# A trunk layer on one Trainium2 core: the ninth pair's up products as seven products, one side's sums kept behind the last head, and the eleventh pair's low parts by DMA

## The chip, the cores and the metric

The kernel runs on one NeuronCore of a Trainium2 chip. The core's engines work side by side, each through its own queue in order: TensorE (PE) multiplies matrices, with PEld its weight loads; VectorE (DVE) does elementwise work; ScalarE (ACT) copies, scales and applies functions; GpSimd (POOL) does small elementwise work and issues some transfers; SyncE (SP) issues most DMA transfers. Engines wait for each other by semaphores. SBUF is the on-chip memory of 128 partitions, PSUM the small memory that TensorE writes, DRAM the memory outside.

The metric is the time of one execution in microseconds. Before the change three runs took 644.28 to 644.42 us, median 644.31.

## The reference

One decoder layer over 512 tokens of width 1024, in float32: forgetting attention with 16 heads, a layer norm, a feed-forward part whose gate passes a causal convolution, a second layer norm, and a gated embedding. The part that is changed is the feed-forward part:

```
def conv_ffn(x, w_up, conv_w, conv_b, w_down):
    u, g = jnp.split(x @ w_up, [FFN_DIM], axis=-1)
    g = causal_dwconv(g, conv_w, conv_b)
    return (jax.nn.gelu(g, approximate=False) * u) @ w_down
```

FFN_DIM is 2816, that is 22 blocks of 128 columns. All blocks, and the 16 heads before them, are computed in both kernels.

## The kernel before, in words

**Split products.** Every float32 operand is cut into a high part (a copy in TensorE's rounded format, whi, xh, written by ACT at L123) and a low part (the operand minus the high part, wlo, xl, written by VectorE at L129). Each product is three matmuls: high with high, high with low, low with high (`three`, L147). The weights pass through class `Weights` (L64): a unit is 1024 columns per partition; `load_to` loads it into a buffer called raw from SP's queue (some units go into a spare piece of another tile, shown as side in the trace), `cut_to` cuts it into whi and wlo, five buffers of each, and `get` asks for a unit and cuts up to four units ahead. With by_dma set (L124), ACT writes the negated high part into wlo, and a DMA from POOL's queue adds the weights to it; VectorE has no part in it.

**Attention.** `scores` (L540) makes a head's probabilities in a tile pr of 1280 columns, of which there are two, used in turn; `turn` (L578) transposes them on TensorE, `values` (L593) multiplies with the values. In the last steps, `out_first` (L615) starts the output projection. `keep_load` and `keep_sums` (L474, L488) work beside the heads: they load the two blocks of up weights of one pair and side, make four sums of them on VectorE, and store those in a DRAM tile called kept, for use in the feed-forward part.

**Feed-forward part.** The 22 blocks f are taken in pairs j = f // 2, counted from 0 here as in the code: j = 8 is the ninth pair, j = 10 the eleventh. A plain pair takes four products of 1024x128 weights with 512 tokens: gate and up (g and u, q = 0 and 1) for each of two blocks. A pair in UP_PAIRS is treated as a 2x2 block matrix product, which by Strassen's method in Winograd's form needs seven products of blocks instead of eight; `up_step` (L836) has the four steps st 0 to 3 for each side, with matmuls of 256 tokens. Its operands are sums of weight blocks. They are either made on VectorE when the weights come in (t12, t3, t4 at L199 to L225) or, for a pair in KEPT, loaded ready-made from the kept tiles. Step 0 leaves a sum in PSUM; VectorE adds a saved part to it (L866), and only then may step 1 write the same PSUM bank again.

**Down products.** The products E of a pair are cut into operands for the down product, which is also done in Strassen's form for three pairs at a time (parts 0 to 2: pairs 0 to 2, 3 to 5, 6 to 8). `operand_sums` (L892) makes four sums on VectorE, `operand_parts` (L904) the high and low parts a, b and s. For a pair j whose successor is in APART, these stand inside the next pair (L990 to L993), otherwise at the pair's own end. The twelve chunks of a part's down product are done between the steps of the following three pairs; CHUNKS says how many chunks stand in which slot. Chunks of part 2 stand in pairs 9 and 10.

**What sets the order.** From f = 2 to the end of the loop, VectorE and ACT run in an order written out by hand (L971); in the rest, and on the other engines, a scheduler of the framework sets the order from priorities and its own costs. The trace's PE names: g and u for the up products, x, y and z for the down products' PSUM banks, o for values, ao and ap for the output projection.

## Time and profile before

| | |
|---|---|
| median of the runs | 644.31 us (644.28 to 644.42, 3 runs) |
| the profiled execution's own time | 644.6 us |
| its span, first to last instruction | 642.9 us |
| TensorE busy | 636.6 us |
| VectorE busy | 540.7 us |
| ScalarE busy | 389.4 us |
| GpSimd busy | 129.1 us |
| mean granted TensorE clock | 0.999 |

In a row of a timeline stand the start and the duration in us, the engine, the line, the operation, out<-in, and the shape; in brackets, how long the engine was idle before, and what ended that. A row of the chain of waits has the start, the time and the engine with what it wrote, several equal ones merged. A row of the windows gives each engine's busy time with its number of instructions in the order PE, PEld, DVE, ACT, POOL, then the granted clock, the DMA share and GB/s. Buffer numbers are left out of the names.

### The profile page before, as it was taken

To read this page: it belongs to the slowest core of one execution; us is meant where nothing else is said; L and a number is where in the kernel's file an instruction comes from. 1 tells how busy PE (TensorE), PEld (TensorE's weight loads), DVE (VectorE), ACT (ScalarE), POOL (GpSimd) and SP (SyncE) were. 2 spreads that over 40 slices of the span, in tenths; PEclk is the share of its full clock that TensorE was granted. 3 is DMA by queue.
4 is the path that set the end of the run, shared out by engine and by line. 5 is a ranking of instruction groups with operands and counts; after the bars stand their busy time and mean duration, and the time that the engine had idled before them with its cause. 6 is when DMAs were issued, how large, how long until landed. Compare 5 with 4: busy or idle time off the path is not lost.

```text
span 642.9 us, 10251 instructions
## 1 busy us (share of the span) xinstructions
PE 636.6 (99%) x3707; PEld 562.4 (87%) x3707; DVE 540.7 (84%) x864; ACT 389.4 (61%) x690; POOL 129.1 (20%) x149
## 2 busy tenths in 40 slices
PE   9999999999999999999999999999999999999997
PEld 7899888888888889989999999999988998888886
DVE  7577779988888689857889989999986998599996
ACT  6273787877785316956666566756644455236872
POOL 2000464454456043110000000102020001002001
PEclk9999999999999999999999999999999999999999
DMA  8766634554588777694676868675854774662632
GB/s 316 249 225 211 220 105 166 175 193 152 181 280 295 269 258 204 147 252 137 197 224 154 239 183 275 189 234 168 255 152 123 207 246 100 181 232 73 221 108 98
DMA packets 51666, 126.87 MB, mean 197 GB/s; under 512 B 5088, under 2 KB 8160, under 8 KB 51616
## 3 DMA queue, kind: packets, MB, share of 16 engines
q1 hardware_dynamic: 46384, 111.93, 52.1%
q0 software_dynamic: 5088, 14.16, 11.3%
q8 instruction: 29, 0.48, 0.3%
q14 instruction: 21, 0.17, 0.1%
q10 hardware_dynamic: 144, 0.13, 0.1%
HBM read 111.39 MB, written 20.97 MB: 206 GB/s over the span
## 4 chain that ended last, share of the span: by engine, by line
PE 92%; DVE 4%; issue 1%; DMA 1%; POOL 0%; SPq 0%; ACT 0%; DVEq 0%; POOLq 0%
PE u L152 17%; PE g L152 17%; PE pp L152 13%; PE x L152 8%; PE pl L152 7%; PE pv L152 7%; PE z L152 4%; PE r L152 3%; PE o L600 3%; PE ao L152 3%; PE t L587 3%; PE y L152 2%; PE s L550 2%; PE s L552 2%; PE p L152 1%
## 5 line engine op out<-in xcount | busy, mean ns | idle before, releaser
L123 ACT ACTIVATE whi<-raw 128x1024 fp32r<-128x1024 f32 (+4 forms) x131 | 128.9, 987 | 92.2 <-PE pv L152 18.4
L129 DVE TENSOR_TENSOR wlo<-raw,whi 128x1024 fp32r<-128x1024 f32 (+4 forms) x126 | 141.7, 1129 | 26.7 <-ACT whi L123 26.0
L574 POOL TENSOR_SCALAR pr<-pr,rl 128x128 f32<-128x128 f32 (+1 forms) x64 | 75.6, 1197 | 74.7 <-DVE rl L570 74.7
L283 POOL COPY neghalf<-neghalf 128x1 f32<-128x1 f32 x16 | 9.6, 601 | 244.3 <-ACT neghalf L282 244.3
L152 PE MATMUL g<-x1h,whi 128*128 128x256 f32 (+1 forms) x164 | 51.7, 315 | 0.0
L152 PE MATMUL g<-x1l,whi 128*128 128x256 f32 (+1 forms) x164 | 51.6, 315 | 0.0
L152 PE MATMUL g<-x1h,wlo 128*128 128x256 f32 (+1 forms) x164 | 51.5, 314 | 0.0
L152 PE MATMUL pp<-xh,wlo 128*128 128x512 f32 (+1 forms) x130 | 50.5, 390 | 0.0
L152 PE MATMUL pp<-xh,whi 128*128 128x512 f32 (+1 forms) x130 | 50.5, 388 | 0.1
L152 PE MATMUL pp<-xl,whi 128*128 128x512 f32 (+1 forms) x130 | 50.4, 388 | 0.0
L152 PE MATMUL u<-x1l,whi 128*128 128x256 f32 (+1 forms) x156 | 50.1, 321 | 0.0
L152 PE MATMUL u<-x1h,wlo 128*128 128x256 f32 (+1 forms) x156 | 50.1, 321 | 0.0
L152 PE MATMUL u<-x1h,whi 128*128 128x256 f32 (+1 forms) x156 | 50.1, 321 | 0.0
L566 ACT ACTIVATE pr<-s,nm 128x128 f32<-128x128 f32 (+1 forms) x64 | 33.6, 527 | 11.8 <-DVE nm L562 11.7
L152 PEld LDWEIGHTS g<-x1h,whi 128*128 128x128 f32 x164 | 31.2, 191 | 2.4 <-issue 0.4
L152 PEld LDWEIGHTS g<-x1l,whi 128*128 128x128 f32 x164 | 31.2, 190 | 2.1
L152 PEld LDWEIGHTS g<-x1h,wlo 128*128 128x128 f32 x164 | 31.2, 190 | 1.9
L123 ACT ACTIVATE whi<-side 128x512 fp32r<-128x512 f32 (+1 forms) x32 | 26.4, 828 | 9.3 <-DVE side L216 3.8
L152 PEld LDWEIGHTS u<-x1l,whi 128*128 128x128 f32 x156 | 29.7, 190 | 2.4
L152 PEld LDWEIGHTS u<-x1h,whi 128*128 128x128 f32 x156 | 29.7, 190 | 2.3
L152 PE MATMUL g<-xsh,wlo 128*128 128x256 f32 x112 | 31.7, 283 | 0.0
L152 PE MATMUL u<-xsh,whi 128*128 128x256 f32 x112 | 31.7, 283 | 0.0
(637 smaller groups left out, 1927.7 us busy)
## 6 DMA issues: line engine op xcount, KB each, us to landing
raw<-wup SPq DMA_DIRECT2D x30, 512.0 KB, 4.8
raw<-wdn SPq DMA_DIRECT2D x26, 512.0 KB, 4.8
raw<-wqk SPq DMA_DIRECT2D x14, 512.0 KB, 3.9
ka<-wup SPq DMA_DIRECT2D x10, 512.0 KB
kb<-wup SPq DMA_DIRECT2D x10, 512.0 KB, 4.3
kept<-kb SPq DMA_DIRECT2D x9, 512.0 KB, 3.4
kept<-ka SPq DMA_DIRECT2D x9, 512.0 KB
raw<-wo SPq DMA_DIRECT2D x8, 512.0 KB, 5.1
```

The lines of the kernel that those rows point to most:

```text
L123: self.nc.scalar.activation(hi[:, c:e], piece, AF.Copy)
L129: self.nc.vector.tensor_sub(lo[:, c:e], piece, hi[:, c:e].bitcast(F32))
L152: nc.tensor.matmul(ps, lhsT, rhs, start=start and n == 0, stop=stop and n == 2, skip_group_check=on)
L283: with tc.issue_after(nc.gpsimd.tensor_copy(small[:, m + 32:m + 33], small[:, m:m + 1]).ins):
L550: nc.tensor.matmul(ps[:, :n], QA[:, q], KA[:, :n], start=True, stop=False)
L552: nc.tensor.matmul(ps[:, :n], qb[0:68, q], kb[0:68, :n], start=False, stop=True)
L566: nc.scalar.activation(pr[:, off:off + w], ps[:, :w], AF.Exp, bias=nm[:, i:i + 1], scale=-1.0, accum_out=ls[:, i:i + 1])
L574: nc.gpsimd.tensor_scalar_mul(pr[:, off:off + w], pr[:, off:off + w], rl[:, i:i + 1])
L587: nc.tensor.transpose(ps[:, w:w + P], pr[:, o:o + P], ident)
L600: nc.tensor.matmul(ps[:, q0:], V[:, j, h], p[:, o:o + w], start=j == 0 and n == 0, stop=j == NT - 1 and n == 1)
```

## The change

Four things are done together.

1. Pair 8 joins UP_PAIRS: its four plain products become seven products. Its side q = 0 gets a kept tile; its side q = 1 has its weight sums made on VectorE as they come in. `up_units` now chooses kept or not by side.
2. The kept tile of (8, 0) is the eleventh. Its two weight blocks are loaded after the last head's transposes, into the two buffers of the probabilities, its sums are made on VectorE in the round after that, and stored from SP's queue. The store of the tenth kept tile moves with it.
3. APART gains 8 and 9, so the operand sums and parts of pairs 7 and 8 stand inside pairs 8 and 9.
4. Pair 10 joins DMA_PAIRS: the low parts of its four units are made by ACT and a DMA from POOL's queue.

CHUNKS for part 2 changes from one chunk in each of twelve slots to eight of one, none, one, none or two: the slots of a pair of seven products differ from those of a plain pair.

```diff
-CHUNKS = (None, (1,) * 8 + (0, 1, 2, 1), (1,) * 12, (2, 1) * 4)
-UP_PAIRS = (2, 3, 4, 5, 6, 7, 9)
-KEPT = (3, 4, 5, 6, 7)
-DMA_PAIRS = (1, 2)
-APART = (2, 3, 4, 5, 6, 7)
+CHUNKS = (None,) + ((1,) * 8 + (0, 1, 2, 1),) * 2 + ((2, 1) * 4,)
+UP_PAIRS = (2, 3, 4, 5, 6, 7, 8, 9)
+KEPT = [(j, q) for j in (3, 4, 5, 6, 7) for q in range(2)] + [(8, 0)]
+DMA_PAIRS = (1, 2, 10)
+APART = (2, 3, 4, 5, 6, 7, 8, 9)
@@ up_units(j): kept or not by side
+        def second(q):
+            if (j, q) in KEPT:
+                return W.add(kept[j, q][:, 0:4:3, :], inner=512)
+            return unit(f1, q, t12(wup[f0, 1 - q][:, :4], 3 + q))
+
+        def third(q):
+            if (j, q) in KEPT:
+                return W.add([(kept[j, q][:, 2, :], 512), (wup[f1, 1 - q][:, 4:], 512)])
+            return unit(f1, q, t3)
+
+        def fourth(_):
+            open_ = [q for q in range(2) if (j, q) not in KEPT]
...
+                nc.vector.tensor_sub(v, v, b)
...
+            return W.add([(kept[j, q][:, 1, :] if (j, q) in KEPT else wup[f0, 1 - q][:, 4:], 512)
+                          for q in range(2)], make=make if open_ else None)
@@ keep_load
-    def keep_load(queue=nc.sync):
+    def keep_load(queue=nc.sync, last=False):
...
-            ab = (ap.tile([P, UNIT], F32, name=f"ka{j}_{q}", tag="keep", bufs=1),
-                  base.tile([P, UNIT], F32, name=f"kb{j}_{q}", tag="raw", bufs=RAW_BUFS))
+            if last:
+                ab = [ap.tile([P, 10 * P], F32, tag="pr", name=f"k{c}{j}_{q}")[:, :UNIT] for c in "ab"]
+            else:
+                ab = (ap.tile([P, UNIT], F32, name=f"ka{j}_{q}", tag="keep", bufs=1),
+                      base.tile([P, UNIT], F32, name=f"kb{j}_{q}", tag="raw", bufs=RAW_BUFS))
@@ the loop over the heads
-        elif s == 0:
+        else:
             keep_sums()
-            keep_load()
+            if s:
+                keep_load()
...
         if 1 <= h < H + 1:
             turn(h - 1)
+        if h == H:
+            keep_load(last=True)
```

The engines' instructions change by this: TensorE has 168 matmuls of 256 tokens in pair 8 where it had 96 of 512; VectorE's list of rows grows from 858 to 870, ACT's from 614 to 636. The orders at the three places that the prediction speaks of are shown there.

More of the change, by code (lines that the diff above doesn't have):

```diff
@@ L242, in up_units, with make @@
         f0, f1 = 2 * j, 2 * j + 1
-        if j in KEPT:
-            return (lambda q: W.add(wup[f0, 1 - q], inner=P),
-                    lambda q: W.add(kept[j, q][:, 0:4:3, :], inner=512),
-                    lambda q: W.add([(kept[j, q][:, 2, :], 512), (wup[f1, 1 - q][:, 4:], 512)]),
-                    lambda q: W.add([(kept[j, i][:, 1, :], 512) for i in range(2)]))
         def unit(f, q, make=None):
             return W.add(wup[f, 1 - q], inner=P, make=make, by_dma=make is None and j in DMA_PAIRS)
-        return (lambda q: unit(f0, q), lambda q: unit(f1, q, t12(wup[f0, 1 - q][:, :4], 3 + q)),
-                lambda q: unit(f1, q, t3),
-                lambda q: W.add([(wup[f0, 1 - i][:, 4:], 512) for i in range(2)], make=t4(3)))
+        def second(q):
[8 more added lines that the diff above has]
+            open_ = [q for q in range(2) if (j, q) not in KEPT]
+            def make(t):
+                if t is None:
+                    return None
+                v, b = (t[:, open_[0] * 512:open_[-1] * 512 + 512],
+                        aside[0][:, 3 + open_[0]:4 + open_[-1], :].rearrange("p a b -> p (a b)"))
+                nc.vector.tensor_sub(v, v, b)
+                return [t]
+            return W.add([(kept[j, q][:, 1, :] if (j, q) in KEPT else wup[f0, 1 - q][:, 4:], 512)
+                          for q in range(2)], make=make if open_ else None)
+        return lambda q: unit(f0, q), second, third, fourth
     dram = ctx.enter_context(tc.tile_pool(name="dram", bufs=1, space=bass.MemoryType.DRAM))
-    kept = {(j, q): dram.tile([P, 4, 512], F32, name=f"kept{j}_{q}") for j in KEPT for q in range(2)}
+    kept = {(j, q): dram.tile([P, 4, 512], F32, name=f"kept{j}_{q}") for j, q in KEPT}
     gq = {f"t{n}": dram.tile([P, 4, 512], F32, name=f"gt{n}") for n in range(1, 5)}
```

## The prediction

> **What bounds the kernel now.** I read the page first, then TensorE's waits, the windows by stage, the chain in order of time, and the timelines of the engines at the three places where the change moves work.
>
> ```profile
> span 642.9 us, 10251 instructions
> PE 636.6 (99%) x3707; PEld 562.4 (87%) x3707; DVE 540.7 (84%) x864; ACT 389.4 (61%) x690; POOL 129.1 (20%) x149
> ...
> PE warm L339 <- DVE zeros L335: 1.1, 1, 1.1
> PE pv L152 <- DVE wlo L129: 0.3, 1, 0.3
> PE nt L728 <- DVE y L720: 0.2, 1, 0.2
> ```
>
> TensorE (PE) is busy for 636.6 of 642.9 us and waits for other engines three times, 1.6 us together. So a matmul taken out anywhere is worth its time, provided nothing it needs comes late; and whatever comes late costs its lateness in full. How near VectorE (DVE) is to being late shows by stage:
>
> ```profile
> 434.00:464.00 30.00, 30.00 (x209) 28.03 (x208) 28.14 (x38) 19.34 (x32) 3.49 (x4) 1.00 0.72 210
> 464.00:495.00 31.00, 31.00 (x147) 25.77 (x146) 22.59 (x35) 14.01 (x22) 3.80 (x4) 1.00 0.54 157
> 495.00:530.00 35.00, 35.00 (x227) 31.97 (x226) 34.82 (x49) 19.19 (x31) 2.19 (x4) 1.00 0.72 206
> 530.00:563.00 33.00, 33.00 (x147) 27.34 (x146) 23.56 (x29) 13.68 (x20) 2.89 (x4) 1.00 0.55 143
> ...
> 514.01 1.22 DVE L129 TENSOR_TENSOR wlo<-raw,whi 128x1024 fp32r<-128x1024 f32 x1
> ...
> 518.03 2.87 PE g L152 x24
> ```
>
> The four windows are (counting pairs from 0, as the code's j does) pair 7, pair 8, pair 9 and pair 10; the third busy time is DVE's. Pair 8, the one that is changed, is the slack one (22.59 of 31 us); pair 9 behind it has none (34.82 of 35). In pair 9 the low part written at 514.01 is ready at 515.2 and read at 518.03: the lead is 2.8 us.
>
> **The change, part by part.**
>
> *TensorE in pair 8.*
>
> ```profile
> 432.93 2.88 PE g L152 x24
> ...
> 461.18 1.43 PE g L152 x12
> 462.61 1.44 PE u L152 x12
> 464.05 5.47 PE g L152 x24
> ...
> 472.24 5.44 PE u L152 x24
> ...
> 479.04 5.65 PE g L152 x24
> ...
> 486.05 5.44 PE u L152 x24
> ...
> 492.85 2.87 PE g L152 x24
> ```
>
> Four plain products take 5.47 + 5.44 + 5.65 + 5.44 = 22.0 us. As seven products the pair has six steps of 24 short matmuls (2.88) and two of 12 (1.43, 1.44): 6 x 2.87 + 2.87 = 20.1 us. The 5.65 holds 0.2 us of waiting that I expect to stay, so the saving is **1.7 us**. The down products between are the same 6.8 us, so pair 9 starts at 492.85 - 1.7 = 491.1.
>
> *VectorE in pairs 8 and 9.*
>
> ```profile
> 498.48 0.68 DVE L208 TENSOR_TENSOR side<-side 128x512 f32<-128x512 f32 x1
> 499.20 0.69 DVE L209 TENSOR_TENSOR side<-side 128x512 f32<-128x512 f32 x1
> 499.81 1.22 DVE L129 TENSOR_TENSOR wlo<-raw,whi 128x1024 fp32r<-128x1024 f32 x1
> 500.94 0.42 DVE L866 TENSOR_TENSOR E<-g,side 128x256 f32<-128x256 f32 x1
> ...
> 492.32 0.42 DVE L899 TENSOR_TENSOR E<-E 128x256 f32<-128x256 f32 x1
> ...
> 493.80 0.68 DVE L908 TENSOR_TENSOR a8l<-E,a8h 128x512 fp32r<-128x512 f32 x1
> ...
> 467.51 0.69 DVE L812 TENSOR_TENSOR E<-a,E 128x512 f32<-128x512 f32 x1 [0.76 <-ACT a L811]
> ```
>
> From start to start these give 0.60 for 512 elements (0.72 where the next one reads the result), 1.13 for 1024, 0.34 for 256, and 1.48 for the four operand sums. Added in pair 8: three more low parts (3.4; seven units instead of four), the four sums of the side that isn't kept (2.5), four adds of the new steps (2 x 0.34 + 2 x 0.60 = 1.9). That is 7.8 on 22.6 in 29.3 us: the slack is gone, and DVE leaves the pair about 1.2 us late. What is worse is the order: pair 8's operand sums and parts (3.8 us) now stand inside pair 9.
>
> VectorE's order at the end of pair 8 before (E_5172 holds that pair's products, a8l is a low part of it):
>
> ```order
> L812 TENSOR_TENSOR E_5172<-a_5310,u_5320 128x512
> L899 TENSOR_TENSOR E_5172<-E_5172 128x256
> L900 TENSOR_TENSOR E_5172<-E_5172 128x256
> L901 TENSOR_TENSOR E_5172<-E_5172 128x256
> L902 TENSOR_TENSOR E_5172<-E_5172 128x256
> L908 TENSOR_TENSOR a8l<-E_5172,a8h 128x512
> ```
>
> And in the change (with its own line numbers), where pair 9's own parts (raw, side, wlo) come first; u_5588 is its up side in PSUM:
>
> ```order
> L208 TENSOR_TENSOR raw_5508<-raw_5508,side 128x512
> L209 TENSOR_TENSOR side<-raw_5508 128x512
> L129 TENSOR_TENSOR wlo_5592<-side,whi_5591 128x512 x2
> L922 TENSOR_TENSOR E_5258<-E_5258 128x256
> L923 TENSOR_TENSOR E_5258<-E_5258 128x256
> L924 TENSOR_TENSOR E_5258<-E_5258 128x256
> L925 TENSOR_TENSOR E_5258<-E_5258 128x256
> L889 TENSOR_TENSOR side<-u_5588,side 128x256
> L931 TENSOR_TENSOR a8l<-E_5258,a8h 128x512
> ```
>
> The sums moved from right behind the product to behind three more units of pair 9, and the add out of u_5588, without which TensorE may not overwrite that bank in pair 9's second up step, moved behind the sums. Ahead of what is shown, after the product, stand three other pairs of L208/L209, the low parts of three units and the add for g. From the end of the product to the end of the add I count four L208/L209 pairs (5.4), four low parts (1.13 + 3 x 1.2), two adds (0.34 + 0.42) and the sums (1.48): 12.4 us. In pair 7 the product ended at 468.20, 4.15 after the next pair's start at 464.05; here that is 495.2, plus the 1.2 of lateness 496.4, and the add ends at 508.8. TensorE gets there after g (2.87), two down chunks (5.44), u (2.88), g (2.87) and ten first matmuls of the next chunks (2.27): 491.1 + 16.3 = 507.4. So it **waits 1.4 us** (bounds: 0.2 without lateness, 2.6 with twice as much).
>
> *The low part by DMA at the head of pair 10.* ScalarE's (ACT's) order there before, whi_5737 being the first unit of pair 10:
>
> ```order
> L123 ACTIVATE whi_5681<-raw_5615 128x1024
> L123 ACTIVATE whi_5712<-side 128x1024
> L803 ACTIVATE a_5732<-E_5388,cw 128x512
> L123 ACTIVATE whi_5737<-raw_5634 128x1024
> L881 ACTIVATE E_5388<-g_5389 128x256
> ```
>
> and now, with pair 10's first unit in whi_5773 and wlo_5774:
>
> ```order
> L123 ACTIVATE whi_5736<-side 128x512
> L123 ACTIVATE whi_5756<-side 128x1024
> L123 ACTIVATE whi_5773<-raw_5671 128x1024
> L125 ACTIVATE wlo_5774<-raw_5671 128x1024
> L123 ACTIVATE whi_5807<-raw_5706 128x1024
> ```
>
> The subtraction has left VectorE (four of 1.13, 4.5 us, in a stage that has 9 us of slack: worth nothing); in its place stand a copy on ACT and, behind it, a DMA from POOL's queue that adds the weights to it. Pair 1 and 2 do this now:
>
> ```profile
> L126 POOL DMA_DIRECT2D wlo<-wup x6: 853/864/960, 252.2 to 279.2; - x6
> ...
> DMA to landing us min/median/max: 7.0/8.9/9.2
> ...
> 261.70 1.04 ACT L125 ACTIVATE wlo<-raw 128x1024 fp32r<-128x1024 f32 x1
> ...
> 263.15 0.87 POOL L126 DMA_DIRECT2D wlo<-wup  x1 [10.03 <-ACT wlo L125]
> ...
> 529.24 0.40 PE L152 MATMUL g<-x1h,whi 128*128 128x512 f32 x1
> 529.48 0.40 PE L152 MATMUL g<-x1l,whi 128*128 128x512 f32 x1
> 529.71 0.39 PE L152 MATMUL g<-x1h,wlo 128*128 128x512 f32 x1
> ```
>
> From the end of ACT's copy (262.74) to the issue is 0.4 us, from the issue to the landing 7.0 to 9.2. There the units are used some 5.4 us apart and the DMA has time; here the unit follows pair 9's short steps. When is the copy made? whi_5756 waits for the last sums of pair 9 (1024 elements, on VectorE). From the add's end VectorE has a8l, b8l, s8l (2.1), two sums of 512 (1.2), three low parts (3.5), four y adds (2.4), an L208/L209 pair (1.3) and that sum (1.1): 11.6, hence 520.4 from 508.8. Three ACT rows of about 1.0 follow: 523.4; issue 523.8. Asked for one by one, the six landed after 9.2, 7.0, 7.4, 9.1, 9.2 and 8.7 us, 8.4 on the mean: landing at **532.2** (530.8 to 533.0). TensorE wants the low part with the third matmul, at 529.71 - 1.7 + 1.4 = 529.4. It **waits 2.8 us** (bounds 1.4 and 3.6; zero if the DMA took 5.6 us or less). What happens on VectorE before hardly changes this sum: a shorter wait in pair 9 lengthens this one. The second low part is copied four ACT rows (4 us) after the first and used 10.9 us after it (a product of 5.44, two chunks of 2.72), so it has 6.9 us more, and the two behind it follow products of 5.44 in the same way: nothing.
>
> [...]
>
> *Behind the last head.* VectorE before (o_2441 is head 15):
>
> ```order
> L591 TENSOR_TENSOR PTl_398<-t_3_2388,PTh_396 128x384
> L607 TENSOR_TENSOR o_2403<-o_2394,o_2403 64x512
> L129 TENSOR_TENSOR wlo_2536<-raw_2427,whi_2535 128x1024
> L607 TENSOR_TENSOR o_2403<-o_2441,o_2403 64x512
> L610 TENSOR_TENSOR ol<-o_2403,oh 128x512
> ```
>
> and now (o_2452 is head 15, ka_0 and kb_0 the blocks of pair 8's kept side):
>
> ```order
> L627 TENSOR_TENSOR o_2408<-o_2399,o_2408 64x512
> L516 TENSOR_TENSOR ka_0_2395<-kb_0_2396,ka_0_2395 128x512
> L517 TENSOR_TENSOR kb_0_2396<-kb_0_2396 128x512
> L518 TENSOR_TENSOR kb_0_2396<-kb_0_2396,ka_0_2395 128x512
> L129 TENSOR_TENSOR wlo_2547<-raw_2438,whi_2546 128x1024
> L519 TENSOR_TENSOR ka_0_2395<-ka_0_2395,kb_0_2396 128x512
> L627 TENSOR_TENSOR o_2408<-o_2452,o_2408 64x512
> ```
>
> ```profile
> 209.92 0.49 PE L587 MATMUL t<-ident,pr 128*128 128x128 f32 x3
> ...
> 219.86 0.68 DVE L607 TENSOR_TENSOR o<-o,o 64x512 f32<-64x512 f32 x1 [2.54 <-ACT o L606]
> ...
> 221.32 0.91 PE L152 MATMUL ao<-whi,oh 128*128 128x512 f32 x3
> ...
> kb<-wup SPq DMA_DIRECT2D x10, 512.0 KB, 4.3
> ...
> side<-wup SPq DMA_DIRECT2D x8, 512.0 KB, 5.3
> ```
>
> The new sums sit in front of head 15's last add, which had 2.54 us of idle time ahead. They wait for kb_0, whose buffer is free when the ten transposes from 209.92 end, at 211.3. With 4.3 us to land, 215.6; three sums, the low part and the last sum take 3.8 (0.72 + 2 x 0.60 + 1.13 + 0.72), so VectorE is free at 219.4, before 219.86. With 5.3 it is 0.5 us late, and TensorE with it, since the matmuls at 221.32 follow at once. I take **0.2 us** (0 to 0.6). The two stores behind it on SP delay loads whose use lies past 255 us: nothing.
>
> **Sum:** -1.7 + 1.4 + 2.8 + 0.2 = **+2.7**. The profiled execution took 644.6 us (1.7 around its span of 642.9, which stay), so it would take 647.3; the median of the runs lies 0.3 below that execution, so the forecast is **647.0 us**.
>
> **Rivals.**
> - *The low part is in time.* It must land within 5.6 us. For it: the DMA engines' share around 524 us is 0.72, and an emptier queue may serve it sooner. Against: six of six measured are slower. Then -1.7 + 1.4 + 0.2 = -0.1: 644.2, no change. [...]
> - *VectorE keeps up too, and the time falls by the matmuls saved.* For it: pair 7 runs without a wait at 28.14 of 30 us busy, with the same order of steps. Against: pair 9 had 34.82 of 35 before it got 3.8 us more. 644.3 - 1.7 = 642.6, faster. It decides where the add ends by 507.4 and the low part lands by 528.
> - *The sums behind the last head come late in earnest.* The load lands as late as the 6.6 us of y<-x2d, and 1.8 us are lost there instead of 0.2: 648.6.
>
> ```profile
> y<-x2d SPq DMA_DIRECT2D x4, 512.0 KB, 6.6
> ```
>
> **How the numbers follow.** 0.2% (1.3 us) is about what a measurement of this kernel tells from no change. Forecast 0.70 (slower; its own range is 645.4, a landing of 7.0 us with nothing lost behind the last head, to 648.2, one of 9.2 with 0.6 lost there; 0.06 of it lies within 0.2%), low part in time 0.14 (same), all in time 0.07 (faster), late sums 0.09 (slower). Slower 0.73, same 0.20, faster 0.07. The range takes in the case of no change and that of the late sums and leaves out the faster one: 643.9 to 648.9.
>
> **What would show it.** Steps g and u of pair 8 at 2.87 us; a wait of TensorE for VectorE's L889 before pair 9's second u step, about 507; a wait of 2 to 4 us for the DMA on wlo inside pair 10's first g product, and pair 10 starting 0 to 1 us earlier than 529.24 but ending later; no wait at 221. Wrong would be: no wait on the DMA in pair 10, landings far from 7 to 9 us there, or a wait in a place I don't name.

## The result and the profile after

The changed kernel takes **653.81 us** (median of 4 runs, 653.38 to 654.86); the kernel before, run beside it, 644.37. The ratio is 1.0146, with a 95% interval of 1.0133 to 1.0159: 9.4 us slower, where I had forecast 2.7 and a range that ended at 648.9. In the profiled executions the span goes from 642.9 to 652.4 us. TensorE's list of waits in the changed kernel names the places:

```profile
PE g L152 <- DMA wlo<-wup: 4.8, 1, 4.8
PE nt L751 <- DVE y L743: 2.7, 2, 2.5
PE u L152 <- DVE side L889: 1.3, 1, 1.3
PE warm L356 <- DVE zeros L352: 1.1, 1, 1.1
PE x L152 <- ACT a8h L930: 0.3, 1, 0.3
PE x L152 <- DVE y L728: 0.2, 1, 0.2
```

The first and the third line are the two waits of the forecast. The second, 2.7 us in the first normalisation, is in a place that I did not name. How much each stage gained or lost shows by TensorE's first matmul of pair 8, of pair 9, of pair 10, and of the down product behind pair 10's first step. In the timeline of before:

```profile
463.89 0.40 PE L152 MATMUL g<-x1h,whi 128*128 128x512 f32 x1
...
492.69 0.28 PE L152 MATMUL g<-x1h,whi 128*128 128x256 f32 x1
...
529.24 0.40 PE L152 MATMUL g<-x1h,whi 128*128 128x512 f32 x1
...
534.71 0.39 PE L152 MATMUL x<-whi,s6h 128*128 128x512 f32 x1
```

and of the changed kernel:

```profile
466.56 0.28 PE L152 MATMUL g<-x1h,whi 128*128 128x256 f32 x1
...
494.02 0.28 PE L152 MATMUL g<-x1h,whi 128*128 128x256 f32 x1
...
532.80 0.40 PE L152 MATMUL g<-x1h,whi 128*128 128x512 f32 x1
...
544.69 0.39 PE L152 MATMUL x<-whi,s6h 128*128 128x512 f32 x1
```

| stretch | before | after | difference | forecast |
|---|---|---|---|---|
| up to pair 8 | 463.89 | 466.56 | +2.67 | +0.2 |
| pair 8 | 28.80 | 27.46 | -1.34 | -1.7 |
| pair 9 | 36.55 | 38.78 | +2.23 | +1.4 |
| pair 10's first step | 5.47 | 11.89 | +6.42 | +2.8 |
| the rest, to the end of the span (not explained) | 108.2 | 107.7 | -0.5 | 0 |

*Pair 10's first step.* In the timelines of the changed kernel, ScalarE's copy, GpSimd's issue and TensorE's wait:

```profile
526.03 1.04 ACT L125 ACTIVATE wlo<-raw 128x1024 fp32r<-128x1024 f32 x1
...
527.48 0.88 POOL L126 DMA_DIRECT2D wlo<-wup  x1 [10.38 <-ACT wlo L125]
...
538.24 0.79 PE L152 MATMUL g<-x1h,wlo 128*128 128x512 f32 x1 [4.81 <-DMA wlo<-wup]
```

The transfer in its chain of work:

```profile
527.48 10.71 DMA wlo<-wup
```

And three windows of it, with the granted clock third from the end and the share of the DMA engines second from the end:

```profile
534.00:538.00 4.00, 0.00 (x0) 0.00 (x0) 3.49 (x6) 1.60 (x3) 0.00 (x0) 0.96 1.06 303
538.00:542.00 4.00, 3.76 (x11) 3.00 (x12) 2.12 (x3) 2.73 (x4) 0.94 (x1) 0.61 0.80 219
542.00:546.00 4.00, 4.00 (x19) 3.34 (x18) 1.59 (x3) 1.11 (x2) 0.97 (x2) 1.00 0.57 57
```

The transfer takes 10.7 us, of which 5.95 us pass before TensorE needs it, and TensorE stands idle for 4.81. The DMA engines are full in the last four us of it (a share of 1.06 from 534 to 538 us); over its whole length their share is 0.91. Then TensorE's clock is halved for a while: it is granted 0.61 in 538 to 542 us and makes 11 matmuls there, 0.43 us from start to start at first, and 19 in the next four, 0.23 apart. That is the other 1.6 us of the 6.42.

*The first normalisation.* Six rows in order of time: the load of the convolution's rows, two of GpSimd's gate copies, GpSimd's power (the step that raises the variance to the power of -1/2), VectorE's scaling, TensorE's transposes.

```profile
225.06 0.33 SPq L720 DMA_DIRECT2D cw<-cwb  x1
...
235.25 0.72 POOL L291 DMA_DIRECT2D gt<-wg  x1 [1.92 <-issue]
...
239.01 0.69 POOL L291 DMA_DIRECT2D gt<-wg  x1 [2.84 <-issue]
...
239.72 0.58 POOL L739 TENSOR_TENSOR mv<-mv,neghalf 128x1 f32<-128x1 f32 x1
...
240.34 1.28 DVE L743 SCALAR_TENSOR_TENSOR y<-y,mv,b 128x1024 f32<-128x1024 f32 x1 [2.88 <-POOL mv L739]
...
248.16 1.09 PE L751 MATMUL nt<-ident,y 128*128 128x128 f32 x8 [2.47 <-DVE y L743]
```

Two issues in GpSimd's queue stand for 1.92 and 2.84 us; the power is queued behind them, VectorE waits 2.88 us for the power, and TensorE 2.47 us for VectorE some tiles later. In the kernel before the same load was issued at 222.07. What stands ahead of all this is in the changed kernel's chain of work, at the end of the late tile's second store:

```profile
219.90 4.20 DMA kept<-ka
224.10 0.91 issue
225.01 1.29 DVE st L733 x2
```

The normalisation's first statistics (st) begin only when that store has ended, at 225.01 us; before they began at 223.95.

### The profile page after: what moved, and what is told of

It is laid out like the page before. It is cut to its first block, busy times and chain, and to the rows that moved or that the text cites. A ratio compares the mean times of both kernels' runs of the same rounds, so it can differ in the third digit from the quotient of the medians.

```text
span 652.4 us, 10461 instructions
## 1 busy us (share of the span) xinstructions
PE 637.8 (98%) x3779; PEld 566.1 (87%) x3779; DVE 546.7 (84%) x876; ACT 399.5 (61%) x712; POOL 134.9 (21%) x153
## 4 chain that ended last, share of the span: by engine, by line
PE 83%; DVE 8%; DMA 4%; issue 4%; POOL 1%; ACT 0%; DVEq 0%; ACTq 0%; POOLq 0%; SPq 0%
PE u L152 15%; PE g L152 15%; PE pp L152 14%; PE pv L152 7%; PE pl L152 7%; PE x L152 6%; PE r L152 3%; PE z L152 3%; PE t L607 3%; PE o L620 3%; DVE wlo L129 2%; PE ao L152 2%; PE s L570 2%; DMA wlo<-wup 2%; PE s L572 2%
## 5 line engine op out<-in xcount | busy, mean ns | idle before, releaser
L123 ACT ACTIVATE whi<-raw 128x1024 fp32r<-128x1024 f32 (+4 forms) x134 | 131.4, 985 | 86.9 <-PE pv L152 17.7
L152 PE MATMUL u<-x1l,whi 128*128 128x256 f32 (+1 forms) x152 | 47.3, 311 | 0.0
L152 PE MATMUL u<-x1h,wlo 128*128 128x256 f32 (+1 forms) x152 | 47.3, 311 | 0.0
L152 PE MATMUL u<-x1h,whi 128*128 128x256 f32 (+1 forms) x152 | 47.2, 311 | 0.0
L152 PE MATMUL u<-xsh,whi 128*128 128x256 f32 x128 | 36.3, 284 | 1.3 <-DVE side L889 1.3
L152 PE MATMUL g<-xsh,wlo 128*128 128x256 f32 x128 | 36.2, 283 | 0.0
L152 PE MATMUL u<-xsl,whi 128*128 128x256 f32 x128 | 36.2, 283 | 0.0
L152 PE MATMUL g<-xsl,whi 128*128 128x256 f32 x128 | 36.2, 283 | 0.0
L152 PE MATMUL u<-xsh,wlo 128*128 128x256 f32 x128 | 36.2, 283 | 0.0
L152 PE MATMUL g<-xsh,whi 128*128 128x256 f32 x128 | 36.2, 282 | 0.0
L123 ACT ACTIVATE whi<-side 128x512 fp32r<-128x512 f32 (+1 forms) x33 | 27.0, 821 | 10.7 <-DVE side L208 3.1
```

The costliest lines, as they stand in the source:

```text
L123: self.nc.scalar.activation(hi[:, c:e], piece, AF.Copy)
L152: nc.tensor.matmul(ps, lhsT, rhs, start=start and n == 0, stop=stop and n == 2, skip_group_check=on)
```

## Experiments

All ratios are to the kernel before, run on the same chip. Its medians beside these runs were 644.1 to 644.6.

### Pair 10's low parts

**The transfers taken out of the change.**

```diff
-DMA_PAIRS = (1, 2, 10)
+DMA_PAIRS = (1, 2)
```

> The changed kernel, but the eleventh pair's four low parts are made by VectorE again, as before. Theory A (the first of these transfers lands too late, and nothing else of it costs): TensorE's wait of 4.8 us and the 1.6 us of slow clock behind it go, so 653.8 - 6.4 = 647.4 us, 646.9 to 647.9; TensorE's list of waits shows nothing over 0.5 us ahead of the eleventh pair, and the clock is 1.00 there. Rival B (VectorE is full in the last third, and its subtraction is as late as the transfer was): a wait for VectorE of 3 us or more takes its place, 650 us or more. Rival C (moving the parts off VectorE also shortened the tail, where the changed kernel won 0.5 us): 647.4 + 0.5 = 647.9.

Measured: 648.68 us, 1.0062 (1.0043 to 1.0081). The profiled execution, at 648.6, has no wait in pair 10; 5.1 us are gone by the medians. Pair 10's first step is 5.47 us again. The forecast of 647.4 was low because this kernel loses more in the normalisation than the changed one did in its profile: behind a wait of 2.50 us there the clock is halved as well, as in the kernel with the late tile alone below (the transposes at 248.30 us take 1.80 us, 1.09 in the changed kernel, and the matmuls of 256 tokens behind them start 0.21 us apart until 251.8, then 0.12). VectorE makes these parts in time, so rival B falls.

**The transfers alone, in the kernel before.**

> The kernel before, with one line changed: the eleventh pair's four low parts by DMA. Theory A: the issue stands some 5.6 us ahead of TensorE's need (the prediction's reading of before), and the transfer takes 7.0 to 10.7 us, so TensorE waits 1.4 to 5.1 us; the slow clock follows only a wait that is long enough, 0 to 1.6 us. With the landing of 10.7 us seen in the changed kernel: 644.4 + 5.1 + 1.6 - 0.5 = 650.6; with the mean of 8.4 us: 644.4 + 2.8 - 0.5 = 646.7. Rival D (the late landing is a matter of the other edits, which put more transfers beside it): the landing is 9 us or less and the time under 647.2. If A's longer figure comes out, the length of the transfer is its own and not the ninth pair's doing.

Measured: 646.28 us, 1.0036 (1.0024 to 1.0048). In its timelines, the issue and the wait:

```profile
521.99 0.88 POOL L126 DMA_DIRECT2D wlo<-wup  x1 [12.52 <-ACT wlo L125]
...
531.68 0.50 PE L152 MATMUL g<-x1h,wlo 128*128 128x512 f32 x1 [2.06 <-DMA wlo<-wup]
```

In the chain of work the transfer takes 9.64 us without any of the other edits, so they are not what makes it long, and rival D falls. The wait is 2.06 and the clock stays whole (the matmuls of 512 tokens behind it start 0.23 us apart, as ahead of it). The difference to the changed kernel is the lead, which the expectation had put at 5.6 us (so both of its times came out too high): here the issue stands 7.6 us ahead of TensorE's need (531.68 - 2.06 - 521.99), there 5.95 (538.24 - 4.81 - 527.48), since in pair 9 ScalarE's copy, which waits for VectorE's sums, now runs later against TensorE.

**One transfer, and three.** Does the second transfer, issued 5 us behind the first, slow it down? And are the later three in time?

```diff
-u_up[f, q] = W.add(wup[f, 1 - q], inner=P, by_dma=j in DMA_PAIRS)
+u_up[f, q] = W.add(wup[f, 1 - q], inner=P, by_dma=j in DMA_PAIRS and (j < 10 or (f, q) == (20, 0)))
```

> The changed kernel with only the first of the eleventh pair's four low parts by DMA. Theory S (the landing of 10.7 us is this transfer's own share of full DMA engines, the loads issued between 524 and 532 us): the landing stays at 9.5 to 11 us and TensorE's wait at 3.8 to 4.8 us; time 653.4 to 654.9 plus up to 0.5 for the tail. Rival S2 (the second such transfer, issued 5 us behind the first, takes half of the engines from it): the landing falls to 8.5 us or less, the wait to 2.6 us or less, and the clock stays whole, so the time falls by 2.2 to 3.9 us, to 650 to 651.5.

Measured: 654.69 us, 1.0154 (1.0136 to 1.0171). The transfer took 9.7 us and TensorE waited 3.8, with the clock halved behind it (0.57 granted from 539 to 543 us): the second transfer was not what made the first long. The opposite, three by DMA and the first on VectorE, in the kernel "mended" of below:

> The kernel just described, but the last three of the eleventh pair's four low parts by DMA; only the first, the one that came late, on VectorE. Theory A (only the first transfer is late; behind it the lead of issue over need is a whole step longer): no wait of TensorE over 0.5 us in the eleventh pair, VectorE is freed of three subtractions of 1.2 us, and the tail gains the 0.5 us seen in the changed kernel: 643.7 - 0.5 = 643.2, 642.4 to 644.0. Rival K (each of these transfers takes 8 to 11 us in company, and the second is late too once the first does not hold TensorE back): a wait of 1 to 5 us, 645 to 649.

Measured: 647.35 us, 1.0046 (1.0032 to 1.0060), against 645.59 without them. The second unit was in time, the third was 8.2 us under way and TensorE waited 1.4 us for it, so rival K holds: behind the first step these transfers are not free either, even where 8.2 us is all that one takes.

### The first normalisation

**No late tile.**

```diff
-KEPT = [(j, q) for j in (3, 4, 5, 6, 7) for q in range(2)] + [(8, 0)]
+KEPT = [(j, q) for j in (3, 4, 5, 6, 7) for q in range(2)]
```

> The changed kernel without the sums behind the last head: the ninth pair's seven products take both sides' sums from VectorE while the pair runs. Theory A (the late sums' blocks and stores cost 2.7 us in the first normalisation): the normalisation goes as in the kernel before, TensorE's wait of 2.7 us for VectorE's normalised tile is gone, 653.8 - 2.7 = 651.1, and up to 1.5 us comes back because VectorE makes four sums more in the ninth pair: 650.9 to 652.6. Rival E (the loss in the normalisation comes from the store of the tenth kept tile, which is moved behind the last head's transposes in this kernel too): the wait stays and the time is 653.8 to 655.

Measured: 652.67 us, 1.0128 (1.0113 to 1.0143). TensorE waits for nothing in the normalisation, so rival E falls. Of the 2.7 us only 1.1 arrive at the end: VectorE has four sums more, and in pair 10 the clock was halved for twice as long (0.51 granted from 535 to 541 us).

**The late tile alone, in the kernel before, read by nobody.**

> The kernel before with the eleventh kept tile loaded, summed and stored behind the last head just as in the changed kernel, but with nobody reading it; the ninth pair stays as it was with eight products. Theory A: the whole of the changed kernel's 2.67 us between 221 and 249 us is due to this, 644.4 + 2.7 = 647.1, 646.8 to 647.4, with TensorE's wait of some 2.7 us for VectorE's normalised tile and GpSimd's two issue waits of about 2 and 3 us ahead of the power. Rival F (the loss comes from the other changes of the queues, such as the loads of the ninth pair's weights brought forward): 644.4, within 0.3.

Measured: 648.86 us, 1.0063 (1.0043 to 1.0082). TensorE's transposes in its timeline, and a window behind them:

```profile
249.18 1.94 PE L735 MATMUL nt<-ident,y 128*128 128x128 f32 x8 [2.63 <-DVE y L727]
```

```profile
249.00:253.00 4.00, 3.83 (x19) 3.83 (x20) 4.00 (x7) 3.00 (x5) 0.00 (x0) 0.57 0.79 237
```

The wait is there, 2.63 us, and a half clock behind it (0.57 granted over the four us): the late tile costs 4.3 us by the medians with nothing else changed, and rival F falls.

**Traffic or memory?** First the traffic without the memory:

```diff
+spare = [dram.tile([P, 4, 512], F32, name=f"spare{n}") for n in range(2)]
...
+            for n in (0, 2):
+                nc.sync.dma_start(spare[1][:, n:n + 2, :], spare[0][:, n:n + 2, :])
```

> The kernel before, with as many bytes as the late sums load and store (two transfers of 512 KB, then two more that wait for them) copied from memory to memory at the two places of the queue where the changed kernel loads and stores; no block in the chip's own memory is held, nothing is summed, and nobody reads the copies. Theory M (what costs 2.7 us in the first normalisation is the memory: the probabilities' buffers are given to the next stage's tiles only when the late stores have read them): nothing is held, the loads of the convolution's and the norm's rows are issued within 1 us of 222.1 as before, TensorE waits 0.2 us, 644.4 to 645. Theory T (it is the traffic: the transfers of 219 to 236 us stand in line behind one another, so GpSimd's gate copies land later and their successors cannot be issued): TensorE waits 2 to 3 us for VectorE's normalised tile, and the slow clock of 1.6 us follows in some executions: 646.9 to 648.9, as the kernel with the late sums and no reader.

Measured: 643.68 us, 0.9997 (0.9988 to 1.0006), no wait of TensorE, and the rows' load at 222.04. But the run does not try what it was meant to: nothing in the program made these transfers wait, and in the trace all four stand near the start of the kernel, the loads at 22.65 and 27.20 us, the copies at 39.07 and 43.07. The first copy in SP's timeline:

```profile
39.07 0.49 SPq L673 DMA_DIRECT2D spare<-spare  x1
```

So theory T, the traffic, stays open. Then the memory without the attention's pool:

```diff
-ab = [ap.tile([P, 10 * P], F32, tag="pr", name=f"k{c}{j}_{q}")[:, :UNIT] for c in "ab"]
+both = base.tile([P, 8, 512], F32, tag="xl", name="late")
+ab = [both[:, 4 * n:4 * n + 2, :].rearrange("p a b -> p (a b)") for n in range(2)]
```

> The kernel before with the unread eleventh kept tile, its two blocks not in the probabilities' buffers but in the low parts of x (a buffer of the longest-lived pool, free since the last projection), so that the attention's pool can close without waiting for its stores. Theory M' (the first tiles of the next stage wait until everything in the attention's pool has been released, whatever addresses they get; the late stores out of that pool are what delays the convolution's rows, the norm's rows and the statistics): the rows' loads go at about 222 us as before, TensorE's wait for the normalised tile falls to 0.2 us: 644.4 to 645.0. Rival V (the extra sums on VectorE behind the last head, four of 0.69 us, delay the last value sums and so the normalisation, wherever the blocks lie): 646.7 to 649.4, as with the blocks in the probabilities' buffers.

Measured: 645.43 us, 1.0020 (1.0009 to 1.0032). The load of the convolution's rows in SP's timeline, and TensorE's wait for the normalised tile in its list:

```profile
222.61 0.33 SPq L705 DMA_DIRECT2D cw<-cwb  x1
```

```profile
PE nt L736 <- DVE y L728: 0.2, 1, 0.2
```

The wait is down to 0.2 us: 3.1 of the 4.3 us are gone, about 1.2 us stay. But two things changed at once. With a buffer that is free all along the scheduler also made the tile earlier; its two stores are issued from 205.91 us on, where the kernel with the blocks in the probabilities' buffers issues them at 219.07 and 220.81:

```profile
205.91 0.80 SPq L480 DMA_DIRECT2D kept<-late  x2
```

So this run does not tell the place from the time. In the profile 0.7 us are lost ahead of pair 8 and 0.8 inside it (464.58 and 29.61 us against 463.89 and 28.80); why is open. Who waits for the stores is named outright in the next kernel.

**The late tile a head earlier.**

```diff
-            if s == 0 and h != 2:
+            if s == 0 and h != 2 or h == H - 1:
...
```

> The changed kernel with the eleventh kept tile loaded in the slot of the last head but one (into the usual two buffers, not the probabilities'), its sums and stores in the slot where the kernel before has those of the tenth. Theory A: neither the memory nor the transfers of 218 to 226 us are in the way any more, TensorE waits 0.2 us in the first normalisation, and the sums of the tenth tile, made a head earlier, find VectorE free enough: 653.8 - 2.7 = 651.1, 650.5 to 651.8. Rival G (the sums moved a head earlier hold up the last heads' masks and operands): TensorE loses 0.5 to 2 us between 190 and 221 us, 651.6 to 653.1.

Measured: 653.52 us, 1.0146 (1.0130 to 1.0162): no gain. By the profile TensorE reaches pair 8 at 466.87 us, as late as in the changed kernel (466.56): its wait in the normalisation is down to 1.6 us, but it waits another 1.0 us at 222.7. The tile takes the usual buffers, whose first is in the attention's pool as well, and has to wait for the tenth tile's stores to free it; its own stores then go at 223.5 and 224.7 us, later than in the changed kernel. VectorE's timeline:

```profile
229.00 2.47 DVE L730 BATCH_NORM_STATS2 st<-y 128x6 f32<-128x512 f32 x4 [0.49 <-DMA kept<-ka]
```

The first statistics of the normalisation wait for the store of the kept tile, with which they have nothing to do. Their tiles belong to the pool that is opened when the attention's is closed, and in this kernel they begin 4.30 us behind the issue of the last store out of the old one (224.70). Across all kernels the load of the convolution's rows, the first of the new pool, was issued at 221.8 to 222.6 us where no late tile lay in the attention's pool, and at 225.1 to 229.0 where one did. In all seven of the latter the load went 4.3 to 6.1 us behind the issue of the late tile's last store, which took 4.20 us in the changed kernel.

**GpSimd's queue.** The last six gate copies issued behind all four powers:

```diff
-        for _ in range(2 if t < 3 else 0):
-            copies.send(st[:, 1, :1])
+    for _ in range(6):
+        copies.send(st[:, 1, :1])
```

> The changed kernel with the last six of GpSimd's gate copies issued behind all four of the norm's powers, not between them. Theory P (GpSimd's own queue carries the delay: the power stands behind two issues that waited 1.92 and 2.84 us): the power goes within 1 us of its inputs, TensorE's wait of 2.5 us falls under 1.2 us (what is left is VectorE's later start of 1.1 us), and the slow clock behind it cannot come: 653.8 - 1.3 to 653.8 - 2.7, 651.1 to 652.5. Rival Q (VectorE itself is late, since its statistics waited for the memory, and the power only follows it): the wait stays at 2 us or more, 653.3 to 654.9.

Measured: 655.33 us, 1.0171 (1.0146 to 1.0196). Two rows of TensorE's timeline:

```profile
247.45 1.09 PE L751 MATMUL nt<-ident,y 128*128 128x128 f32 x8 [0.70 <-DVE y L743]
...
274.81 0.50 PE L152 MATMUL g<-x1h,wlo 128*128 128x512 f32 x1 [1.75 <-DMA wlo<-wup]
```

The wait falls from 2.47 to 0.70 us, so the queue does carry most of the delay; why its issues stand longer here than before is not shown, and the stores' traffic is not ruled out. The time did not follow: the copies now stand ahead of pair 1's low parts in the same queue, and TensorE waits 1.75 us there, and 0.8 us for ScalarE (oh) ahead of the normalisation. It reaches pair 8 at 467.90 us, 1.3 later than in the changed kernel.

### Pair 9

**Three things mended.** The first mend on VectorE's order put the add of pair 9's up side ahead of pair 8's operand sums:

```diff
+            if amid is not None and j != 9:
                 amid()
             nc.vector.tensor_add(c1 if j in APART else e[:, :HALF], x, c1)
+            if amid is not None and j == 9:
+                amid()
```

> The changed kernel with three things undone or moved: the eleventh pair's low parts on VectorE again, the eleventh kept tile a head earlier as above, and in the ninth tail pair (counted from 0) VectorE's add ahead of the operand sums of the pair before, so that the add is not queued behind four sums. Theory A: the terms are separate, so what is left is the saving of the ninth pair's seventh-eighth, 1.5 to 1.7 us less than before, and of the tenth pair's wait at most 0.4 us: 644.4 - 1.5 + 0.4 = 643.3, 642.6 to 643.8, faster than before. Rival B (VectorE has no room: what the sums gain by waiting, the operand parts lose, and TensorE waits 1 us or more at the next step of that pair): 643.9 to 645.

Measured: 647.71 us, 1.0055 (1.0038 to 1.0073). The early tile still held up the normalisation (a wait of 2.0 us; 2.7 us lost ahead of pair 8), which is the larger part of the miss. The other is pair 9: the wait for the add is gone, waits of 0.6 and 0.4 us stand in its place, and the pair takes 38.35 us, 1.8 more than before, where the sum had 0.4. With the tile in the longest-lived pool instead (and so made earlier, as above):

> The changed kernel with the late tile's two blocks in that same buffer of the longest-lived pool, the eleventh pair's low parts on VectorE, and the tenth pair's add ahead of the operand sums. Theory M': the normalisation goes as before, so that what is left is 1.5 to 1.7 us saved in the ninth pair, less what was seen of VectorE in the tenth and eleventh pairs of the kernel with three things mended (waits of 0.6 and 0.4 us): 644.3 - 1.6 + 1.0 = 643.7, 643.0 to 644.4. Rival V: the normalisation still costs 2 to 4 us: 645.5 to 648.

Measured: 645.59 us, 1.0021 (1.0012 to 1.0030). The three places that I had found are mended, and it is still 1.4 us slower than the kernel before. By TensorE's first matmuls, it is 0.97 us behind at the start of pair 8 (the late tile alone, in the same buffer, lost 0.7 there), pair 8 takes 27.36 us (1.44 saved) and pair 9 takes 38.63 (2.08 lost). VectorE at the end of pair 8 before, in a window (its busy time is the third) and in its timeline:

```profile
470.00:492.70 22.70, 22.70 (x101) 18.51 (x101) 15.97 (x21) 9.53 (x14) 3.80 (x4) 1.00 0.60 174
```

```profile
491.60 0.69 DVE L812 TENSOR_TENSOR E<-a,u 128x512 f32<-128x512 f32 x1 [2.20 <-PE u L152]
```

and in the mended kernel, where pair 9 starts at 492.22:

```profile
470.00:492.20 22.20, 22.15 (x157) 20.68 (x156) 21.36 (x32) 14.36 (x24) 1.13 (x3) 1.00 0.85 243
```

```profile
497.41 0.69 DVE L836 TENSOR_TENSOR E<-a,E 128x512 f32<-128x512 f32 x1 [0.76 <-ACT a L835]
```

Before, VectorE was busy for 16.0 of 22.7 us, had waited 2.20 us for TensorE, and made pair 8's last product 1.1 us ahead of pair 9's start. Now it is busy for 21.4 of 22.2 and makes that product 5.2 us behind it. Not all of this is lateness. In a pair of seven products the last product always comes after the pair's last step: in the kernel before, pair 7's is made at 467.51 us, 3.6 behind pair 8's start at 463.89, and TensorE waits for nothing there. Only the other 1.6 us are lateness, near the 1.2 us of the forecast. The difference is that pair 8 was then a plain pair, with room on VectorE. Over both pairs, before and in the mended kernel:

```profile
463.89:529.24 65.35, 65.35 (x368) 57.23 (x367) 56.76 (x83) 33.20 (x52) 5.99 (x8) 1.00 0.63 182
```

```profile
464.86:530.85 65.99, 64.98 (x441) 59.32 (x439) 63.13 (x91) 39.78 (x70) 5.26 (x8) 1.00 0.70 199
```

Before, VectorE had 8.6 us of the 65.35 to spare. Now it is busy for 63.13 of 65.99, and the stretches of more than 0.1 us in which it waits for ScalarE add up to another 2.5. So VectorE's own work with these waits takes 65.6 us, more than the 63.9 that TensorE would need (65.35 - 1.44).

**Is it the order or the amount?** Order first, by putting pair 8's operand sums, then pair 7's too, back behind their own pairs:

```diff
-APART = (2, 3, 4, 5, 6, 7, 8, 9)
+APART = (2, 3, 4, 5, 6, 7, 8)
```

> The mended kernel (late tile's blocks in the longest-lived pool, the eleventh pair's low parts on VectorE), with the operand sums of pair 8 right behind pair 8, as in the kernel before, and not inside pair 9. Theory O (it is the order: the sums and low parts stand inside pair 9 where TensorE waits for the add and the low parts): pair 9 takes 36.6 us as before in place of 38.6, 645.6 - 2.0 = 643.6, 643.0 to 644.2. Theory W (it is the amount: VectorE has no gap from 489 to 529 us in either order): pair 9 keeps 38 us or more, or what it gives back pair 8 takes, 645.0 to 646.2.

> The same with the operand sums of pair 7 right behind pair 7 too, so that both stand where the kernel before has them. Theory O: 643.6, as the run before or better by up to 0.4. Theory W: 645.0 to 646.5; VectorE is then behind already at the start of pair 8, and TensorE waits there for the low parts.

Measured: 645.58 us, 1.0017 (1.0009 to 1.0026), pair 9 at 38.54 us; and 648.30 us, 1.0060 (1.0047 to 1.0074), pair 9 at 38.41 with a new wait of 2.6 us inside pair 8 and a halved clock behind it (0.81 granted from 474 to 478 us, 0.76 from 478 to 482; matmuls 0.21 us apart in place of 0.12 from 476.6 to 479.9). Theory O falls: with pair 8's sums behind pair 8, TensorE waits 1.2 us for a low part in pair 9 instead. Then more work for VectorE, both sides' sums in pair 8:

> The changed kernel without the late tile (both sides' sums of pair 8 by VectorE while it runs), without transfers for the eleventh pair, with pair 8's operand sums right behind it. Compared with the first of these runs VectorE makes three sums of 0.69 us more in pairs 8 and 9. Theory W: each us of VectorE's work there costs TensorE about its length: 2 us more than the first run's time, less 0.5 to 1.0 that the late tile costs in the attention: 646 to 647.5. Theory O: the same time as the first run's within 0.5.

Measured: 646.49 us, 1.0032 (1.0020 to 1.0044), pair 8 at 28.68 us and pair 9 at 38.98: the three extra sums (2.0 us more of VectorE's time) cost TensorE 1.9 us in the two pairs, as theory W has it; by the medians about 1 us of that is won back by having no late tile. Then less work:

> The mended kernel (add ahead of the sums), with the low parts of pair 8's operands, three subtractions of 0.7, 0.4 and 1.2 us on VectorE, left out and copies by ScalarE in their place, so that part of the down projection is computed with other numbers; the order of the rest is unchanged. Theory W: pair 9 shortens by what TensorE waits there for VectorE, some 2 us: 36.6 us, 645.6 - 1.2 to 645.6 - 2.0, 643.6 to 644.4. Theory O, or ScalarE as the next bound: the waits stay or move to ScalarE, 645.1 to 646.

Measured: 645.17 us, 1.0010 (1.0001 to 1.0019), pair 9 at 38.12 us. In VectorE's timeline:

```profile
512.62 0.69 DVE L129 TENSOR_TENSOR wlo<-raw,whi 128x512 fp32r<-128x512 f32 x1 [1.99 <-ACT whi L123]
```

Of the 2.3 us that VectorE saved it lost most again, waiting 1.99 us for ScalarE, which made the copies ahead of this high part. It begins this row 0.5 us earlier than in the mended kernel (513.17, shown below), and pair 9 is 0.5 us shorter: a small relief, and it arrived. So GpSimd, which is busy for 2.8 of the 38.7 us of pair 9 in the mended kernel, got the low parts: the largest (spare marks pair 8's parts), then all three (the condition is spare alone).

```diff
-            nc.vector.tensor_sub(l, src, h.bitcast(F32))
+            if spare and src.shape[1] == 4:
+                nc.gpsimd.tensor_sub(l, src, h.bitcast(F32))
+            else:
+                nc.vector.tensor_sub(l, src, h.bitcast(F32))
```

> The mended kernel with the largest of the three low parts of pair 8's operands (1.23 us on VectorE) made by GpSimd; the result is the same. It is needed last of the three, and GpSimd, whose scaling of 128x512 took 1.59 us in the kernel before, has it done some 3 to 4 us behind its high part. Theory W (amount): VectorE's adds and low parts behind it come 1.1 us earlier, TensorE's two waits in pair 9 (0.4 and 0.6 us) go, 645.6 - 1.0 = 644.6, 643.9 to 645.1. Rival: the wait moves to GpSimd's result or to ScalarE, 645.1 to 646.6.

> The same with all three low parts by GpSimd (2.3 us of VectorE). Theory W: VectorE is 2.3 us ahead, but the first low part, needed at 511.0 us of the mended kernel and begun at 510.2, takes GpSimd 1.6 us or more, so TensorE waits about 1 us for it: 645.6 - 1.5 + 1.0 = 645.1, 644.0 to 645.6. Rival (GpSimd's work on two operands slows VectorE or is itself far longer than its scaling): 645.6 to 648.

Measured: 646.83 us, 1.0035 (1.0022 to 1.0048), pair 9 at 39.10; and 647.56 us, 1.0044 (1.0031 to 1.0057), pair 9 at 40.48. In the first of them, TensorE's waits and GpSimd's row in the timeline:

```profile
PE x L152 <- DVE y L729: 1.9, 2, 1.6
...
PE u L152 <- DVE E L903: 0.3, 1, 0.3
```

```profile
511.50 2.62 POOL L935 TENSOR_TENSOR s8l<-E,s8h 128x1024 fp32r<-128x1024 f32 x1 [12.58 <-ACT s8h L933]
```

GpSimd needs 2.62 us for what takes VectorE 1.23, and a wait of 1.6 us for an add of the down product comes up where those of 0.4 and 0.6 shrink to one of 0.3. Theory W's gain did not come, but VectorE was not relieved either. In the same kernel, VectorE's subtraction beside GpSimd's, and the same one in the mended kernel:

```profile
511.97 2.70 DVE L129 TENSOR_TENSOR wlo<-raw,whi 128x512 fp32r<-128x512 f32 x1
```

```profile
513.17 0.69 DVE L129 TENSOR_TENSOR wlo<-raw,whi 128x512 fp32r<-128x512 f32 x1
```

In this kernel it takes 2.0 us longer and ends 0.55 us behind GpSimd's, so VectorE lost more than the 1.23 us that it had been spared. With all three low parts on GpSimd two such stretches take 2.90 and 2.48 us instead of 1.28 and 0.69: 3.4 us lost for 2.3 spared. The rival of that run, that GpSimd's work slows VectorE, holds.

What ties these runs together is VectorE's add of pair 9's up side (L903, at 528.57 us in the mended kernel), for which TensorE waits ahead of the pair's last step. In the mended kernel and the three behind it (ScalarE's copies, one low part on GpSimd, three) the add starts 36.35, 35.84, 36.83 and 38.20 us into pair 9, and the pair takes 38.63, 38.12, 39.10 and 40.48 us: 2.27 to 2.28 us more each time.

So pair 9 took 38.1 to 40.5 us in every kernel in which pair 8 is made as seven products, with the sums in either place. In these four it is as long as VectorE takes to reach that add. That the amount of VectorE's work is the cause is shown by its full time over the two pairs, by the run with more work, whose 2.0 us cost 1.9, and by these four. How much less work would bring back the 36.55 us is not shown: no run gave VectorE more than 0.5 us.

## Why the prediction was wrong

The direction was right and the size was not. Point by point:

- **TensorE in pair 8, -1.7:** it measured -1.34. The steps took 2.88 us as forecast; one took 3.22 us with the wait behind it, where the sum had allowed 0.2 us of waiting, and the rest of the difference is open.
- **VectorE in pair 9, +1.4:** the wait is where it was put and nearly as long (1.27 us):

```profile
512.02 0.42 DVE L889 TENSOR_TENSOR side<-u,side 128x256 f32<-128x256 f32 x1
...
512.49 0.39 PE L152 MATMUL u<-xsh,whi 128*128 128x256 f32 x1 [1.27 <-DVE side L889]
```

  But the stage lost 2.23 us. The other 1 us is lost just ahead of that row, where TensorE goes through the first matmuls of three chunks:

```profile
508.86 0.50 PE L152 MATMUL x<-whi,a8h 128*128 128x512 f32 x1 [0.35 <-ACT a8h L930]
```

  ScalarE made this high part of pair 8's product 0.4 us ahead of pair 9 before (492.32) and makes it 14 us into pair 9 now (508.19). And with the wait for the add removed others came up, and the pair still lost 2.1. The step that failed is pricing one late instruction: VectorE's work fills the two pairs (63.13 of 65.99 us busy in the mended kernel), so whatever stands next in its queue, or in ScalarE's behind it, comes late instead.
- **The low part by DMA, +2.8:** it measured +6.42. The lead was right (5.6 us forecast, 5.95 measured). The landing was mis-sized: 8.4 us as the mean of six transfers, 10.7 here and 9.5 to 10.4 in five other kernels, all above the highest of the six (9.2). What makes it longer is open. Full DMA engines alone do not explain it: of the six, one took 9.20 us at a share of 0.72 (252.17 to 261.37 us) and one 9.15 at 1.04 (275.59 to 284.74), against 10.71 at 0.91 here. One profile also showed too little of the spread: the same six took 7.9 to 10.0 us in the changed kernel's. And a consequence was missing: behind this wait TensorE's clock was halved (0.61 granted from 538 to 542 us), another 1.6 us. No later wait took this back, as the transfers taken out show (-5.1 us).
- **Behind the last head, +0.2:** on VectorE this was right: the add of head 15 starts at 219.90 us instead of 219.86, and TensorE does not wait at 221 us. The step that failed is the sentence on the stores: "delay loads whose use lies past 255 us: nothing". I asked what is queued behind the stores on SP, and not what waits until they have read their buffers. That was the next stage's pool, whose first statistics start 1.06 us later (225.01 against 223.95), and behind it GpSimd's queue, which carries most of TensorE's wait: 2.67 us in the changed kernel, 4.3 where the clock fell too. What makes the issues in that queue stand stays open.
- **The rivals:** the third (late sums, 648.6) named the right tile and the wrong mechanism: its load was in time (it landed at 215.80 us, where the sum had 215.6), and what came late was the freeing of its buffers, at the end of its last store (224.10 us). The first, a low part in time, needed a landing within 5.6 us; at this place the landings took 9.5 to 10.7.
- **A version that pays:** none was found. With these places mended the seven products save 1.4 us in pair 8, and pair 9 loses 2.1.

## What to carry to other kernels

The late tile's last store took 4.20 us from its issue, and the next stage's first statistics came behind its end: before a buffer near the end of a stage is used once more, ask which pool it belongs to and what opens when that pool closes. Price a transfer that has no time to spare from the slowest of its like, and from more than one profile, not from the mean of one (8.4 us was the mean of six here, 9.2 the slowest of them, 10.7 came). Where an engine is busy for nearly all of a stage, as VectorE was in pair 9 (36.10 of 36.50 us before), work added in the stage ahead of it is likely to cost in this one (2.1 us in the mended kernel), and mending the wait that shows may only bring up the next (0.6 and 0.4 us in place of 1.27). Before work that was moved to another engine is read as relief, look whether the first engine's rows beside it have kept their length (0.69 us became 2.70). And before a run is read as an answer, look in its trace whether the instruction stands at the time where it was meant to.

## What the runs showed of the hardware

**TensorE's clock fell after short waits.** Between 100 and 600 us of all these kernels' profiles no idle time of TensorE up to 2.06 us was followed by a lower clock. Of five between 2.47 and 2.63 us, four were (2.50, 2.58 and twice 2.63); all five between 3.6 and 4.8 us were (3.64, 3.81, 3.84, 4.47 and 4.81). Matmuls of 512 tokens then started 0.42 to 0.43 us apart in place of 0.22 to 0.24, those of 256 tokens 0.21 to 0.22 in place of 0.12; a window wholly inside such a stretch, 537 to 541 us of the kernel with the gate copies behind the powers, shows 0.50 granted. The lost clock amounts to a half clock for 3.4 us (changed kernel, 0.04 x 4 + 0.39 x 4 = 1.72 us lost, twice that at half speed; the same in the kernel with the late tile alone, 0.43 x 4) or for twice that, in the windows of the kernel without a late tile:

```profile
531.00:535.00 4.00, 0.16 (x2) 0.01 (x1) 3.53 (x6) 1.60 (x3) 0.08 (x1) 0.88 1.03 289
535.00:541.00 6.00, 6.00 (x14) 4.74 (x15) 4.09 (x5) 2.73 (x4) 1.91 (x2) 0.51 0.68 185
```

So a wait of 2.5 us cost either 2.5 us, once, at 2.47, or 4.2 with the lower clock, four times, at 2.50 to 2.63. What decides between the two was not shown.

**GpSimd's issues stood.** In the changed kernel two of the gate copies' issues stood for 1.92 and 2.84 us for which the profile names nothing that they waited for; in the kernel before the longest was 1.27. What holds them was not tried.

**GpSimd's subtractions held up VectorE's.** In each of the three stretches in which GpSimd subtracted one tile from another (2.62 us; 1.66 and 1.18 in a row; 2.41), the subtractions that VectorE began meanwhile ended 0.54 to 0.55 us behind GpSimd's and took 1.6 to 2.0 us longer than elsewhere. Beside GpSimd's scaling of the probabilities, which multiplies one tile by a column, VectorE's subtractions kept their length (0.74, 0.69 and 0.68 us for 128x512 at 103.10, 103.88 and 104.48 us of the kernel before, beside GpSimd's 5.24 us from 102.58). For other kinds of GpSimd's work no row is given here.
